# Four of eight k-tile pairs with seven block products in the gate/up projections of a decoder trunk, alternating with pairs of eight

## The chip, the cores and the metric

One Trainium2 chip, one core. The metric is the device time of one execution in microseconds; of several executions of a kernel the median is given. Before the change it is 1897.59 us, the median of three (1898.46, 1897.59 and 1895.63).

## The reference

One layer of a hybrid decoder trunk on 256 tokens of width 2048, all in float32. A combined input projection, three token mixers and their merge come first, then a SwiGLU feed-forward block, a per-layer embedding term and a last norm. The change lies in the feed-forward block alone:

```python
h = rms_norm(x, g_ffn[i])
gate, up = jnp.split(h @ w_gate_up[i], 2, axis=-1)     # 2048 x (2 * 5632)
x = x + (jax.nn.silu(gate) * up) @ w_down[i]           # 5632 x 2048
```

## The kernel before, in words

**Precision.** TensorE multiplies in float32r. Each float32 operand is split in a high and a low part (`whi`, `wlo` for weights), and a product takes three matmuls, high by high, high by low and low by high (`three`, lines 243 to 246). The weights stream from HBM once. ScalarE (ACT) writes the high part (L216) and VectorE (DVE) subtracts it from the raw weights for the low part (L228). There is a second way for the low part (L220, L221): ACT writes the negative of the high part into `wlo`, and a DMA issued on GpSimd's queue (POOL) adds the raw weights to it from HBM, an accumulating transfer of 512 KB, called "an accumulate" below. It saves VectorE a subtraction and costs ACT a copy and the DMA engines a second reading of those weights.

**Quads.** The gate/up projection runs in 11 quads (class `Quad`), numbered 0 to 10 below; the places of the pairs in a quad are numbered from 0 as well. A quad makes 512 columns of gate and the 512 columns of up that belong to them, for both halves of the tokens: a product of 2 x 2 blocks (token half by gate or up) over 16 k-tiles, taken in eight pairs of k-tiles. A pair of kind "o" takes the eight block products, that is 24 matmuls of 128x512, from two split weight pieces. A pair of kind "s" takes the same result with seven products, 21 matmuls, in Winograd's form: sums and differences of the blocks stand for the blocks. Its price is four VectorE additions on the raw weights (L276 and L236) and four split pieces, three whole and one of half size, instead of two. The kinds are in `PAIRS = "soosooso"`: three "s", five "o", 183 matmuls and 8 transposes a quad. The first quad goes through its pairs in an order of its own (`START`), since its last stationary tiles come late. In every "o" pair the piece of the up columns is finished by an accumulate, but for the first four places of the first quad: 52 accumulates in all.

**Groups.** After three quads (in the last group two) come four down products of 12 (8) k-tiles each, on the activations `aT` that the quads of the group left. So a group is three quads of some 42.5 us each and 66 us of down products.

**Buffers and order.** Raw weights have six buffers (`raws`), split pieces seven for each part (`wparts`, in `Flow`: `RAWS, PARTS = 6, 7`). A load starts when an earlier raw tile has been split, and a piece is split when TensorE has done with an earlier piece. The class `Flow` writes each engine's instructions in an order that it plans from costs of its own: 0.681 a product, 1.2 a split, 0.62 an addition, and 8.0 (`ADDED`) that TensorE is to allow an accumulate. `room` decides whether a piece may still be taken, `do_split` allots its buffers and emits. The scheduler beneath may then move instructions of one engine past one another. Each engine works off its own instructions strictly in order. A pool of 13 big tiles (`t8`, 8 KB a partition) holds the two tiles of the residual stream, the eight stationary tiles `st` of the quads, and up to three `aT`. While a group's first quad runs, none of its `aT` is in use yet.

**Evacuation.** The seven accumulators of a quad are merged on ACT and DVE when the next quad starts: a copy (`ga`, L1332), additions on `vx` and `ga` (L506), sigmoids (`gs`, L1345), and then transposes to `aT`. The results of a down product are added to the residual stream `xr` (L506).

Of the kernel before, what the change touches and what calls it, by code (L numbers as in the profile page):

```python
# [11 lines left out]
F32R = mybir.dt.float32r  # L12
# [7 lines left out]
P = 128  # L20
T = 256
D = 2048
NB = 512
# [17 lines left out]
class Group:  # L41
# [6 lines left out]
    def __init__(self, w, kts, c0, n, stat, evac, need=(), pre=None, kind="tok", cost=1.3, key=None):  # L48
        self.w, self.kts, self.c0, self.n = w, list(kts), c0, n
        self.stat, self.evac, self.need, self.pre, self.kind = stat, evac, need, pre, kind  # L50
        self.cost, self.key = cost, key
        self.ps = None
        self.held = []
# [9 lines left out]
class Quad:  # L63
# [6 lines left out]

    def __init__(self, w, c0, c1, pairs, mid, end, order=None, plain=0):
        self.w, self.cs, self.pairs, self.mid, self.end = w, (c0, c1), pairs, mid, end
        self.order = list(order or range(len(pairs)))
        self.plain = plain
        self.ps = {}


# [14 lines left out]
class Piece:  # L94


    def __init__(self, n):
        self.n = n
        self.ops = []
        self.parts = []  # L100
        self.left = 0
# [12 lines left out]
class Flow:  # L114


    RAWS, PARTS = 6, 7
    LAND, GAP, ADDED = 5.0, 1.3, 8.0

    def __init__(self, nc, tc, pools, nm, big, split, quad_parts):  # L120
# [33 lines left out]

    def room(self, piece):
        self.live = [p for p in self.live if p.left]
        return sum(p.n for p in self.live) + piece.n <= self.PARTS

    def next_split(self):

# [10 lines left out]
    def do_split(self, op):  # L171
        if op.piece is not None and op.piece not in self.live:
            p = op.piece
            for part in ("whi", "wlo"):
                p.parts.append([
                    self.pools["wparts"].tile([P, 2, NB], F32R, tag=part, name=self.nm(part)) for _ in range(p.n)
                ])
            self.live.append(p)
        self.emit(self.todo.pop(0))
        for z in op.frees:  # L180
            z.freed = True
            self.slots.append(op.end)
        self.issue()
# [70 lines left out]
    def add_quad(self, g):  # L254
# [2 lines left out]
        first_p, last_p = g.order[0], g.order[-1]  # L257
        for pos, p in enumerate(g.order):
            kind = g.pairs[p]
            r1, r2 = (Load(g.w, 2 * p, c, NB) for c in g.cs)  # L260
            if kind == "s":
                self.loads += [r2, r1]
                pc = [Piece(1) for _ in range(4)]
                x = []

                def new_sum(x=x):
# [9 lines left out]
                        self.nc.vector.tensor_tensor(out=X(0), in0=R2(0), in1=R2(1), op=ALU.add),  # L276
                    ), [], r2,
                )
                b1 = self.split_ops(pc[0], 0, lambda r=r1: r.raw, load=r1)
                t1 = self.add_op(lambda R2=R2: R2(0), lambda R2=R2: R2(0), lambda R1=R1: R1(0), [t3], r1)  # L280
                t2 = self.add_op(lambda X=X: X(1), lambda R2=R2: R2(0), lambda R2=R2: R2(1), [t1], r1)
                self.split_ops(pc[1], 0, lambda r=r2: r.raw, [t1], r2, [r2])
# [15 lines left out]
                              after=(lambda g=g: self.late(g.mid(g, g.ps), g)) if p == last_s and z == "4" else None)  # L298
            else:
                self.loads += [r2, r1]  # L300
                pc = [Piece(1) for _ in range(2)]
                self.split_ops(pc[1], 0, lambda r=r2: r.raw, load=r2, frees=[r2],
                               neg=None if pos < g.plain else g.w[:, 2 * p : 2 * p + 2, g.cs[1] : g.cs[1] + NB])
                self.split_ops(pc[0], 0, lambda r=r1: r.raw, load=r1, frees=[r1])
# [156 lines left out]
def kernel(  # L461
# [284 lines left out]
    w_in_v, w_gu_v, w_dn_v = wv(w_in), wv(w_gate_up), wv(w_down)  # L746
# [510 lines left out]

    PAIRS = "soosooso"  # L1260
    fst = {}

    def quad_stat(p, b, z):
# [160 lines left out]
        return f  # L1424

    NJ = 11
    START = ((1, 2, 0, 4, 3, 5, 6, 7), 4)
    flow.transposes(None, [x_part(3, j) for j in (0, 2)])
    plan = []
    for lo, hi in ((0, 3), (3, 6), (6, 9), (9, NJ)):  # L1430
        for j in range(lo, hi):
            plan.append(Quad(w_gu_v, j * NB, (NJ + j) * NB, PAIRS, quad_mid, quad_end(j), *(START if j == 0 else ())))
        for c in range(4):
            plan.append(Group(w_dn_v, range(4 * lo, 4 * hi), c * NB, NB, blk(aT), ev_down(c, hi == NJ), key="a"))

# [146 lines left out]
```

## Time and profile before

| | us |
|---|---|
| median of three runs | 1897.59 |
| profiled execution | 1896.41 |
| its span in the trace | 1894.6 |
| TensorE busy | 1867.9 (99%) |
| VectorE busy | 1320.2 (70%) |
| ScalarE busy | 1041.1 (55%) |
| quads and down products of the first three groups and the two last quads (1060.77 to 1732.81) | 672.0 |

In the views, PE is TensorE's matmul, PEld its weight load, DVE VectorE, ACT ScalarE, POOL GpSimd's queue and SP the queue of the plain loads. A timeline row has start, duration, engine, line, operation, output <- inputs with their shapes, and in brackets the engine's idle time ahead of it with what ended it. Matmuls are pipelined, so their durations overlap: the distance from one start to the next is what a matmul costs. A row of the windows view has the stretch, its length, each engine's busy time with its instruction count, the granted TensorE clock, the DMA engines' share and the rate in GB/s. A row of a group has busy time and mean ns, then the idle time just ahead and what ended most of it. Times inside the span are from its start. The first quad begins at 1060.77.

### The profile page before, as it was taken

How to read it: one execution, taken by the hardware profiler on the slowest of the kernel's cores; microseconds unless marked ns; L12 is line 12 of the kernel's file. 1: busy time of each engine (PE TensorE's matmuls, PEld its weight loads, DVE VectorE, ACT ScalarE, POOL GpSimd, SP SyncE). 2: the span in 40 equal slices, each digit the busy share in tenths (PEclk: the TensorE clock that was granted, in tenths of full speed). 3: DMA queues.
4: the chain of work that ended last, by engine and by line, in shares of the span. 5: the costliest groups of instructions: out<-in, count | busy, mean ns of one | idle time of the engine just before them, and what ended most of it. 6: DMA issues, size and time to landing. Idle time of an engine off the chain costs nothing.

```text
span 1894.6 us, 23186 instructions
## 1 busy us (share of the span) xinstructions
PE 1867.9 (99%) x8589; PEld 1551.7 (82%) x8589; DVE 1320.2 (70%) x1657; ACT 1041.1 (55%) x1204; POOL 71.7 (4%) x74
## 2 busy tenths in 40 slices
PE   8999999999999999999999999999999999999997
PEld 6888888888888888888888778888888888887887
DVE  6457777668888889655556777758765776676654
ACT  6656556554454435644445666546644665465654
POOL 0000000000000000000000011001100110010000
PEclk9999999999999999999999999999999999999999
DMA  8766556556666656676655599679976997698552
GB/s 311 238 181 186 176 177 190 168 154 178 190 186 193 194 160 211 198 236 189 188 189 167 194 255 263 222 199 259 268 228 192 250 263 239 187 252 277 178 161 95
DMA packets 204401, 390.47 MB, mean 206 GB/s; under 512 B 12432, under 2 KB 21264, under 8 KB 203904
## 3 DMA queue, kind: packets, MB, share of 16 engines
q1 hardware_dynamic: 189248, 358.12, 59.5%
q0 software_dynamic: 15040, 30.87, 9.3%
q8 instruction: 67, 1.10, 0.2%
q14 instruction: 46, 0.38, 0.1%
HBM read 386.85 MB, written 2.10 MB: 205 GB/s over the span
## 4 chain that ended last, share of the span: by engine, by line
PE 92%; DMA 3%; DVE 3%; ACT 1%; issue 1%; SPq 0%; DVEq 0%; ACTq 0%
PE acc L651 17%; PE acc L652 17%; PE acc L650 17%; PE acc L246 12%; PE acc L245 12%; PE acc L244 12%; DMA wlo<-in_w_gate_up_dram 1%; DMA raw<-in_w_gate_up_dram 1%; DVE wlo L228 1%; PE tr L719 1%; PE tr L1287 1%; PE sc L928 1%; DMA x<-in_x_feat_dram 0%; DMA pt<-in_p_feat_dram 0%; DVE raw L236 0%
## 5 line engine op out<-in xcount | busy, mean ns | idle before, releaser
L516 DVE TENSOR_TENSOR wlo<-raw,whi 128x1024 fp32r<-128x1024 f32 (+2 forms) x378 | 450.0, 1196 | 293.9 <-ACT whi L515 293.3
L515 ACT ACTIVATE whi<-raw 128x1024 fp32r<-128x1024 f32 (+2 forms) x378 | 391.2, 1037 | 465.1 <-PE acc L652 391.8
L216 ACT ACTIVATE whi<-raw 128x1024 fp32r<-128x1024 f32 (+1 forms) x333 | 332.3, 1006 | 301.4 <-PE acc L246 267.0
L650 PE MATMUL acc<-whi,hhi 128*128 128x512 f32 (+1 forms) x1120 | 432.7, 387 | 5.5 <-ACT whi L515 5.5
L651 PE MATMUL acc<-wlo,hhi 128*128 128x512 f32 (+1 forms) x1120 | 430.1, 384 | 0.5 <-DVE wlo L516 0.5
L652 PE MATMUL acc<-whi,hlo 128*128 128x512 f32 (+1 forms) x1120 | 430.1, 384 | 0.0
L228 DVE TENSOR_TENSOR wlo<-raw,whi 128x1024 fp32r<-128x1024 f32 (+1 forms) x281 | 318.1, 1144 | 155.6 <-ACT whi L216 154.7
L245 PE MATMUL acc<-wlo,st 128*128 128x512 f32 x671 | 262.1, 391 | 4.1 <-DMA wlo<-in_w_gate_up_dram 3.6
L244 PE MATMUL acc<-whi,st 128*128 128x512 f32 x671 | 262.0, 393 | 1.6 <-DVE xr L506 1.5
L246 PE MATMUL acc<-whi,st 128*128 128x512 f32 x671 | 261.5, 391 | 0.0
L650 PEld LDWEIGHTS acc<-whi,hhi 128*128 128x128 f32 x1120 | 210.8, 188 | 46.5 <-ACT whi L515 5.9
L651 PEld LDWEIGHTS acc<-wlo,hhi 128*128 128x128 f32 x1120 | 210.9, 188 | 41.9 <-DVE wlo L516 1.4
L652 PEld LDWEIGHTS acc<-whi,hlo 128*128 128x128 f32 x1120 | 210.7, 188 | 41.3
L245 PEld LDWEIGHTS acc<-wlo,st 128*128 128x128 f32 x671 | 126.3, 188 | 32.0 <-DMA wlo<-in_w_gate_up_dram 5.0
L244 PEld LDWEIGHTS acc<-whi,st 128*128 128x128 f32 x671 | 126.3, 188 | 29.1 <-DVE xr L506 1.5
L246 PEld LDWEIGHTS acc<-whi,st 128*128 128x128 f32 x671 | 126.4, 188 | 26.4
L244 PE MATMUL acc<-whi,aT 128*128 128x512 f32 x352 | 138.3, 393 | 1.5 <-ACT aT L515 1.5
L245 PE MATMUL acc<-wlo,aT 128*128 128x512 f32 x352 | 137.2, 390 | 0.0
L246 PE MATMUL acc<-whi,aT 128*128 128x512 f32 x352 | 136.6, 390 | 0.0
L509 DVE SCALAR_TENSOR_TENSOR cv<-uT,vec,cv 128x255 f32<-128x255 f32 (+15 forms) x240 | 110.8, 466 | 4.8
L221 POOL DMA_DIRECT2D wlo<-in_w_gate_up_dram x52 | 62.6, 1204 | 819.9 <-ACT wlo L220 485.8
L244 PEld LDWEIGHTS acc<-whi,aT 128*128 128x128 f32 x352 | 66.2, 188 | 15.5 <-ACT aT L515 2.1
(276 smaller groups left out, 2073.7 us busy)
## 6 DMA issues: line engine op xcount, KB each, us to landing
raw<-in_w_in_dram SPq DMA_DIRECT2D x262, 512.0 KB, 3.7
raw<-in_w_gate_up_dram SPq DMA_DIRECT2D x176, 512.0 KB, 5.3
raw<-in_w_down_dram SPq DMA_DIRECT2D x88, 512.0 KB, 5.1
wlo<-in_w_gate_up_dram POOLq DMA_DIRECT2D x52, 512.0 KB, 8.2
raw<-in_w_gla_out_dram SPq DMA_DIRECT2D x32, 512.0 KB, 3.6
raw<-in_w_o_dram SPq DMA_DIRECT2D x32, 512.0 KB, 4.0
raw<-in_w_ple_gate_dram SPq DMA_DIRECT2D x24, 512.0 KB, 3.6
raw<-in_w_sc_out_dram SPq DMA_DIRECT2D x16, 512.0 KB, 4.3
```

Of the source, the lines that this page charges most:

```text
L216: a = self._op("A", cost * 0.88, lambda: nc.scalar.activation(out=hi(), in_=src(), func=AF.Copy), deps, load, piece, frees if neg else ())
L221: nc.gpsimd.dma_start(out=lo(), in_=neg, accum_op=ALU.add)
L228: lambda: nc.vector.tensor_tensor(out=lo(), in0=src(), in1=hi().bitcast(F32), op=ALU.subtract),
L244: pe.matmul(o, lhsT=s[0], rhs=w[0], start=start, stop=False)
L245: pe.matmul(o, lhsT=s[0], rhs=w[1], start=False, stop=False)
L246: pe.matmul(o, lhsT=s[1], rhs=w[0], start=False, stop=stop)
L509: dve.scalar_tensor_tensor(out=o, in0=a, scalar=s, in1=b, op0=op0, op1=op1)
L515: a = act.activation(out=hi, in_=src, func=AF.Copy)
L516: b = dve.tensor_tensor(out=lo, in0=src, in1=hi.bitcast(F32), op=ALU.subtract)
L650: pe.matmul(o, lhsT=shi[:, hs], rhs=whi, start=st, stop=False)
L651: pe.matmul(o, lhsT=shi[:, hs], rhs=wlo, start=False, stop=False)
L652: pe.matmul(o, lhsT=slo[:, hs], rhs=whi, start=False, stop=sp)
```

## The change

`PAIRS` becomes "sosososo": four "s" and four "o" pairs, alternating, 180 matmuls a quad. In every quad but the first, the "s" pairs at places 0 and 2 finish their first piece (the gate columns) by an accumulate instead of VectorE's subtraction (`NEG`). The first quad gets another order of pairs and no accumulate at all (`START`). So there are 60 accumulates, six in each of ten quads. `Piece` gets a number `may`: when the seven ordinary buffers are full, a piece can take a big tile (`wp`, high and low part in one) as long as fewer pieces than `may` are in such tiles. Quads of a group get 3, 2 and 1 for it (`lo + 3 - j`), the first quad of a group from its third place on only.

```diff
-    PAIRS = "soosooso"
+    PAIRS = "sosososo"
...
-    START = ((1, 2, 0, 4, 3, 5, 6, 7), 4)
+    START = ((1, 3, 0, 2, 5, 4, 6, 7), 8)
...
-            plan.append(Quad(w_gu_v, j * NB, (NJ + j) * NB, PAIRS, quad_mid, quad_end(j), *(START if j == 0 else ())))
+            plan.append(Quad(w_gu_v, j * NB, (NJ + j) * NB, PAIRS, quad_mid, quad_end(j), *(START if j == 0 else (None, 0)), lo + 3 - j))
...
+    NEG = (0, 2)
...
-        return sum(p.n for p in self.live) + piece.n <= self.PARTS
+        return self.held(False) + piece.n <= self.PARTS or self.held(True) < piece.may
+
+    def held(self, extra):
+        return sum(p.n for p in self.live if p.extra == extra)
...
+            p.extra = self.held(False) + p.n > self.PARTS
+            if p.extra:
+                b = self.big("wp", (P, 2, 2, NB), F32R)
+                p.parts = [[b[:, 0, :, :]], [b[:, 1, :, :]]]
...
+            may = g.spare if pos > 1 or g.spare < 3 else 0
...
-                pc = [Piece(1) for _ in range(4)]
+                pc = [Piece(1, may) for _ in range(4)]
...
-                b1 = self.split_ops(pc[0], 0, lambda r=r1: r.raw, load=r1)
+                b1 = self.split_ops(pc[0], 0, lambda r=r1: r.raw, load=r1,
+                                    neg=g.w[:, 2 * p : 2 * p + 2, g.cs[0] : g.cs[0] + NB] if pos in self.NEG and not g.plain else None)
```

Three places of the order show what moves. Numbers behind a name only tell tiles apart; line numbers after the change are higher by 11 to 13.

VectorE in the first quad. Before, an "s" pair (from L276 on) with an "o" pair's splits on its two sides:

```order
L228 TENSOR_TENSOR wlo_8453<-raw_8329,whi_8452 128x1024
L228 TENSOR_TENSOR wlo_8459<-raw_8335,whi_8458 128x1024
L276 TENSOR_TENSOR sum_8478<-raw_8365 128x512
L228 TENSOR_TENSOR wlo_8481<-raw_8378,whi_8480 128x1024
L236 TENSOR_TENSOR raw_8365<-raw_8365,raw_8378 128x512
L236 TENSOR_TENSOR sum_8478<-raw_8365 128x512
L236 TENSOR_TENSOR raw_8378<-raw_8378,sum_8478 128x512
L228 TENSOR_TENSOR wlo_8499<-raw_8365,whi_8498 128x1024
L228 TENSOR_TENSOR wlo_8518<-sum_8478,whi_8517 128x1024
L228 TENSOR_TENSOR wlo_8522<-raw_8378,whi_8521 128x512
L276 TENSOR_TENSOR sum_8561<-raw_8456 128x512
```

Now two "s" pairs stand behind one another (the end of the first is shown), and then both splits of an "o" pair:

```order
L239 TENSOR_TENSOR wlo_8442<-sum_8408,whi_8441 128x1024
L239 TENSOR_TENSOR wlo_8450<-raw_8321,whi_8449 128x512
L288 TENSOR_TENSOR sum_8455<-raw_8332 128x512
L239 TENSOR_TENSOR wlo_8458<-raw_8338,whi_8457 128x1024
L247 TENSOR_TENSOR raw_8332<-raw_8332,raw_8338 128x512
L247 TENSOR_TENSOR sum_8455<-raw_8332 128x512
L247 TENSOR_TENSOR raw_8338<-raw_8338,sum_8455 128x512
L239 TENSOR_TENSOR wlo_8478<-raw_8332,whi_8477 128x1024
L239 TENSOR_TENSOR wlo_8491<-sum_8455,whi_8490 128x1024
L239 TENSOR_TENSOR wlo_8498<-raw_8338,whi_8497 128x512
L239 TENSOR_TENSOR wlo_8504<-raw_8368,whi_8503 128x1024
L239 TENSOR_TENSOR wlo_8510<-raw_8381,whi_8509 128x1024
```

The first quad has one such pair more than before, and as many "o" splits on VectorE.

ScalarE ahead of the first accumulate. Before, it belongs to the sixth pair of the first quad (the last row is its negative copy):

```order
L216 ACTIVATE whi_8498<-raw_8365 128x1024
L216 ACTIVATE whi_8517<-sum_8478 128x1024
L216 ACTIVATE whi_8521<-raw_8378 128x512
L216 ACTIVATE whi_8533<-raw_8435 128x1024
L216 ACTIVATE whi_8546<-raw_8450 128x1024
L220 ACTIVATE wlo_8534<-whi_8533 128x1024
```

Now it is the first pair of the second quad, behind the half piece of the first quad's seventh pair (`whi_8625`, which reads the last addition), both pieces of its eighth, and the copy of a finished bank:

```order
L227 ACTIVATE whi_8618<-sum_8585 128x1024
L227 ACTIVATE whi_8625<-raw_8501 128x512
L227 ACTIVATE whi_8631<-raw_8507 128x1024
L227 ACTIVATE whi_8637<-raw_8519 128x1024
L227 ACTIVATE whi_8657<-raw_8580 128x1024
L1345 ACTIVATE ga_8670<-acc_8465 128x512
L231 ACTIVATE wlo_8658<-whi_8657 128x1024
```

The first accumulate has moved some four pairs later, to the start of the second quad.

ScalarE around the start of the third quad of the third group. Before, two accumulates (`wlo_12133` and `wlo_12184`), the second with two other splits between its own split and its copy:

```order
L216 ACTIVATE whi_12132<-raw_12003 128x1024
L220 ACTIVATE wlo_12133<-whi_12132 128x1024
L216 ACTIVATE whi_12161<-raw_12026 128x1024
L1345 ACTIVATE gs_12110<-ga_12103,y_8278 128x512 x2
L216 ACTIVATE whi_12183<-raw_12031 128x1024
L216 ACTIVATE whi_12194<-raw_12051 128x1024
L216 ACTIVATE whi_12208<-raw_12123 128x1024
L220 ACTIVATE wlo_12184<-whi_12183 128x1024
```

Now two as well, each with one split between (`wlo_12172` is that of place 1, `wlo_12235` that of place 2):

```order
L227 ACTIVATE whi_12171<-raw_12066 128x1024
L227 ACTIVATE whi_12192<-raw_12089 128x1024
L231 ACTIVATE wlo_12172<-whi_12171 128x1024
L1358 ACTIVATE gs_12189<-ga_12182,y_8281 128x512 x2
L227 ACTIVATE whi_12234<-raw_12113 128x1024
L227 ACTIVATE whi_12271<-raw_12094 128x1024
L231 ACTIVATE wlo_12235<-whi_12234 128x1024
```

The copy of place 1 now stands behind another split (`whi_12192`), where before the copy followed its own split at once; that of place 2 has one split ahead of it instead of two. In the whole program TensorE has 33 instructions less, VectorE 64 more rows, ScalarE 28 more and POOL 8 more; SP's are as many.

More of the change, by code (lines that the diff above doesn't have):

```diff
@@ L63, with __init__ @@
 class Quad:
-    def __init__(self, w, c0, c1, pairs, mid, end, order=None, plain=0):
+    def __init__(self, w, c0, c1, pairs, mid, end, order=None, plain=0, spare=0):
         self.w, self.cs, self.pairs, self.mid, self.end = w, (c0, c1), pairs, mid, end
@@ L76, in __init__ @@
         self.plain = plain
+        self.spare = spare
         self.ps = {}
@@ L94, with __init__ @@
 class Piece:
-    def __init__(self, n):
+    def __init__(self, n, may=0):
         self.n = n
+        self.may, self.extra = may, False
         self.ops = []
@@ L173, in do_split @@
             p = op.piece
[L174 to L177, printed above, removed]
+            p.extra = self.held(False) + p.n > self.PARTS
+            if p.extra:
+                b = self.big("wp", (P, 2, 2, NB), F32R)
+                p.parts = [[b[:, 0, :, :]], [b[:, 1, :, :]]]
+            else:
+                for part in ("whi", "wlo"):
+                    p.parts.append([
+                        self.pools["wparts"].tile([P, 2, NB], F32R, tag=part, name=self.nm(part)) for _ in range(p.n)
+                    ])
             self.live.append(p)
@@ L300, in add_quad @@
                 self.loads += [r2, r1]
-                pc = [Piece(1) for _ in range(2)]
+                pc = [Piece(1, may) for _ in range(2)]
                 self.split_ops(pc[1], 0, lambda r=r2: r.raw, load=r2, frees=[r2],
```

## The prediction

> **What bounds the kernel now.** I read the page first, then busy time by stage, then TensorE's timeline in the one stage where it falls short.
>
> ```profile
> span 1894.6 us, 23186 instructions
> PE 92%; DMA 3%; DVE 3%; ACT 1%; issue 1%; SPq 0%; DVEq 0%; ACTq 0%
> L245 PE MATMUL acc<-wlo,st 128*128 128x512 f32 x671 | 262.1, 391 | 4.1 <-DMA wlo<-in_w_gate_up_dram 3.6
> L244 PE MATMUL acc<-whi,st 128*128 128x512 f32 x671 | 262.0, 393 | 1.6 <-DVE xr L506 1.5
> ```
>
> TensorE (PE) makes 92% of the chain, so whatever shortens its stream shortens the kernel, as long as nothing else starts to end waits. The third row is the change's own ground: 671 is 11 quads of 61 steps, one low-part matmul each, and 3.6 us is what PE waited there for accumulated low parts. The last row has 1.5 us in which PE waited for VectorE's residual adds. Busy time in four quads and in 20 us of one:
>
> ```profile
> core 0: us, PE busy (x) PEld busy (x) DVE busy (x) ACT busy (x) POOL busy (x), PEclk, DMA share, GB/s
> 1060.77:1108.76 47.99, 44.44 (x188) 35.68 (x188) 42.15 (x59) 35.95 (x46) 3.65 (x3) 0.96 0.74 220
> 1108.76:1151.18 42.42, 42.42 (x192) 35.14 (x191) 34.05 (x43) 30.04 (x33) 5.98 (x5) 1.00 0.95 262
> 1302.20:1344.80 42.60, 42.60 (x192) 35.05 (x191) 34.42 (x44) 29.16 (x32) 6.01 (x5) 1.00 0.94 260
> 1538.65:1581.82 43.17, 42.75 (x192) 35.06 (x191) 31.79 (x38) 28.36 (x30) 4.81 (x4) 1.00 0.96 267
> 1120.00:1140.00 20.00, 20.00 (x90) 16.57 (x89) 13.34 (x17) 13.04 (x13) 3.58 (x3) 1.00 1.01 295
> ```
>
> Quads 1, 4 and 8 take 42.4 to 43.2 us with PE busy throughout; VectorE (DVE) idles 8.2 us in quad 4. Quad 0 takes 48.0, and its DVE is busy 42.15. Why:
>
> ```profile
> 1085.99 0.39 PE L244 MATMUL acc<-whi,st 128*128 128x512 f32 x1
> ...
> 1090.75 0.39 PE L244 MATMUL acc<-whi,st 128*128 128x512 f32 x1
> 1094.32 0.50 PE L245 MATMUL acc<-wlo,st 128*128 128x512 f32 x1 [3.19 <-DMA wlo<-in_w_gate_up_dram]
> ...
> 1095.54 0.63 PE L246 MATMUL acc<-whi,st 128*128 128x512 f32 x1
> 1095.96 0.63 PE L244 MATMUL acc<-whi,st 128*128 128x512 f32 x1
> ...
> 1098.52 0.42 PE L244 MATMUL acc<-whi,st 128*128 128x512 f32 x1
> ```
>
> From 1085.99 to 1090.75 stand 21 matmuls: 0.2267 us each, start to start. Then PE idles 3.19 us for one accumulate, and afterwards starts lie 0.42 apart (the granted clock halves) up to 1098.52, which costs 8 x 0.195 = 1.6. So quad 0 loses 4.8 us to one late landing. The chain has the landings:
>
> ```profile
> 1085.44 8.84 DMA wlo<-in_w_gate_up_dram
> ...
> 1156.41 9.08 DMA wlo<-in_w_gate_up_dram
> ...
> 1543.88 9.41 DMA wlo<-in_w_gate_up_dram
> ```
>
> **Term 1, the products.** Each quad loses one eighth product: three matmuls; 11 quads, 33 matmuls, all on the path: 33 x 0.2267 = -7.5 us. A quad's stream becomes 42.4 - 0.7 = 41.7 us.
>
> **What the added kind costs DVE and ScalarE (ACT).** DVE in the first quad:
>
> ```profile
> 1077.17 0.68 DVE L276 TENSOR_TENSOR sum<-raw 128x512 f32<-128x512 f32 x1
> 1077.77 1.22 DVE L228 TENSOR_TENSOR wlo<-raw,whi 128x1024 fp32r<-128x1024 f32 x1
> 1078.91 0.68 DVE L236 TENSOR_TENSOR raw<-raw,raw 128x512 f32<-128x512 f32 x1
> ...
> 1083.83 0.68 DVE L276 TENSOR_TENSOR sum<-raw 128x512 f32<-128x512 f32 x1
> ...
> 1091.39 0.68 DVE L276 TENSOR_TENSOR sum<-raw 128x512 f32<-128x512 f32 x1
> ```
>
> Between the first two sums lies one whole seven-product pair, back to back: 6.66 us; one full split takes 1.14 (1077.77 to 1078.91). A later quad gets +6.66 for the pair, -1.14 for the eight-product pair that it replaces, and -2.28 for the two splits (positions 0 and 2) that now end in an accumulate: +3.2. DVE in quad 4 goes from 34.4 to 37.6 of 41.7 us. ACT gets 3.5 more activations, loses 3 and adds 2 copies: +2.6, to 31.8 (1.06 us each, a row of term 2). Both are hidden beside PE, cost nothing, and would cost what they exceed 41.7 if their own waits grew.
>
> **Term 2, the first quad.** No accumulate is left in it, so its 3.19 and 1.6 us go. In their place DVE has 6.66 us more: four seven-product pairs instead of three, and eight plain splits as before. Before, DVE reached quad 1's first sum at 1091.39 without a pause; now at 1098.1. The last add of position 6 stands five splits ahead (four of 1.14, one of 0.6): 1092.9. ScalarE's order then has, behind that add, a half split, two full ones, the split for quad 1's first accumulate, the copy of a bank, and the negative copy:
>
> ```profile
> 1537.10 1.32 ACT L1345 ACTIVATE gs<-ga,y 128x512 f32<-128x512 f32 x2
> 1538.85 1.07 ACT L216 ACTIVATE whi<-raw 128x1024 fp32r<-128x1024 f32 x1 [0.43 <-PE acc L246]
> 1540.21 1.06 ACT L216 ACTIVATE whi<-raw 128x1024 fp32r<-128x1024 f32 x1 [0.29 <-PE acc L246]
> 1541.57 1.06 ACT L216 ACTIVATE whi<-raw 128x1024 fp32r<-128x1024 f32 x1 [0.30 <-PE acc L246]
> 1542.54 1.04 ACT L220 ACTIVATE wlo<-whi 128x1024 fp32r<-128x1024 f32 x1
> ```
>
> With 1.06 for a full one, 0.6 for each half-size one (an estimate from the 1.06), and 1.34 from the negative copy's start to the issue (1542.54 to 1543.88), the accumulate is issued at about 1092.9 + 0.6 + 3.2 + 0.6 + 1.34 = 1098.6 and lands, 8.84 later, at 1107.5. PE would want it at its second matmul of quad 1: 1060.77 + 48.0 - 4.8 - 0.7 + 0.2 = 1103.5. So it idles 4.0 us and pays the half clock again: 5.6 us against 4.8. Term 2 = +0.8. The stall is not removed, it moves from the sixth pair of quad 0 to the first pair of quad 1. Its ends: -4.8 (DVE or the landing 4 us faster than these rows, no stall), and +3 (DVE also pauses for ACT). I take the middle because every duration in it is a row of this very stage.
>
> **Term 3, margins of the other accumulates.** A piece is split when a buffer of the seven comes free. For an eight-product pair's accumulate that is two pairs and half of the third ahead of its use: (21 + 24 + 12) x 0.2267 = 12.9 us; for position 0 or 2 it is (21 + 24 + 6) x 0.2267 = 11.6. ACT takes two activations and the issue, 2.4, so 10.5 and 9.2 remain for a landing. In quad 1:
>
> ```profile
> q1 hardware_dynamic: 4392, 8.48, 58.6%
> q0 software_dynamic: 1360, 2.62, 36.2%
> ...
> wlo<-in_w_gate_up_dram POOLq DMA_DIRECT2D x5, 512.0 KB, 8.4
> ```
>
> 8.4 median, and up to 9.41 above: 1.1 us to spare before, about nothing now where no big tile helps. By the order the big tiles serve only from the second group of quads on, and there mostly the first two quads of a group; quads 1 and 2 and the third quads of groups two and three run on seven buffers, or seven and one.
>
> ```profile
> 1105.70 1.28 ACT L1345 ACT_TABLE_LOAD   x1
> ```
>
> - Quad 1: behind the first accumulate's copy (done by 1098.3) ACT's order has two splits, the table load, two sigmoids, a half split, three splits and then the second one's copy: 1098.3 + 2.1 + 1.3 + 1.3 + 0.6 + 3.2 + 1.34 = 1108.1, and 1.5 more (an estimate, between 0 and 3) where the sigmoids wait for DVE: issued at 1109.6, landing (8.84) at 1118.4. PE wants it 37 matmuls after the first, 1107.5 + 1.6 + 8.4 = 1117.5: +0.9; the third one queues behind it, +0.4. Together +1.3, ends 0 and +3.
> - The three third quads: in quad 8 now the copy starts two splits after its own split, is issued 5.2 us into the quad and lands at 14.6. After, position 2 is wanted at (21 + 24 + 6) x 0.2267 + 0.9 for the transposes = 12.4 us, with one split between instead of two: issued at 3.8, landing 8.4 to 9.4: up to 0.8 late. Position 1's is queued behind a split that waits for the last pair of the quad ahead: issued near -0.2, wanted at 7.9, 0.3 to 1.3 late. A stall at one gives time to the other: 0.6 per quad, 1.8, less the 0.4 that PE waits so already (3.6 - 3.19): +1.4, ends -0.4 and +5.
>
> **Term 4, where a group begins.** In DVE's order the residual adds of the last down product stand behind adds of the second seven-product pair, which wait for its load:
>
> ```profile
> 1257.92 0.69 DVE L236 TENSOR_TENSOR raw<-raw,raw 128x512 f32<-128x512 f32 x1 [3.75 <-DMA raw<-in_w_gate_up_dram]
> ```
>
> That pair was the fourth of a quad and is now the third, so its loads are the fifth and sixth instead of the seventh and eighth, and six buffers hold them all: they start without waiting for a buffer of the quad's own. Of the 1.5 us that PE waits for residual adds I take 1.0 as gone: -1.0, ends -1.5 and +1 (another wait ahead of the same adds).
>
> The big tiles themselves cost nothing: each is one that a later aT takes, its first use lies 12 us into its quad, and the old aT is read for the last time before the quad starts. If ACT met one not yet free, everything queued on ACT behind it would wait with it.
>
> **Sum**, against the profiled 1896.4 us (span 1894.6 and 1.8 around it): -7.5 + 0.8 + 1.3 + 1.4 - 1.0 = -5.0. The median of the three runs is 1897.6, the profiled run lies 1.2 under it and inside their spread; against the median the forecast is 1892.6.
>
> **A rule that bears on the landings.** Two stretches, one with DVE full, one not, each with its landing:
>
> ```profile
> wlo<-in_w_gate_up_dram POOLq DMA_DIRECT2D x2, 512.0 KB, 9.0
> 1298.00:1308.00 10.00, 10.00 (x45) 8.07 (x44) 9.83 (x15) 7.40 (x9) 2.41 (x2) 1.00 0.93 260
> ```
>
> ```profile
> wlo<-in_w_gate_up_dram POOLq DMA_DIRECT2D x1, 512.0 KB, 7.0
> 1567.00:1578.00 11.00, 11.00 (x51) 9.09 (x50) 6.17 (x6) 8.13 (x9) 1.20 (x1) 1.00 0.88 245
> ```
>
> DVE busy 98%: 9.0 us; 56%: 7.0, at nearly the same DMA share. A busier DVE goes with later landings, and the change makes it busier. The Trainium skill, SBUF — State Buffer, section "Who interferes with whom", infers that VectorE's tensor_tensor does not hold up descriptors that GpSimd writes. By that the landing would stay at the quiet figure, and the sum would be without the +1.4 of the third quads: -6.4. The trace speaks against it, as far as two stretches can.
>
> **Rivals.**
> - *Full gain*: the accumulate of quad 1 comes in time. Then -7.5 - 4.8, and +1.4 of third quads: about -11, 1886.6. For it: DVE is the only thing late there. Against: the sum of rows, by which it is 4.0 us late. Chance 0.17.
> - *The gain is eaten*: as DVE fills, the landing goes to 9.3 and over everywhere; positions 0 and 2 then miss by 0.5 each in some four quads that have no big tile for them, +4 more: -1, 1896.6. For it: the two stretches. Against: the big tiles give the other quads more time. Chance 0.20.
> - *Slower, DMA becomes the bound*: in quad 1 a load takes 0.586 x 42.42 / 16 = 1.55 us of all engines and an accumulate 0.362 x 42.42 / 5 = 3.07. With six accumulates a quad asks 16 x 1.55 + 6 x 3.07 = 43.2 us of 41.7. Were these shares real occupancy, ten quads would take 43.2: 10 x 0.7 more than now, with term 2 about +8, 1905.6. It decides once a quad's DMA work passes 41.7. Against: at a share of 1.01 PE was busy 20.00 of 20.00 us and 295 GB/s went through, while 22 transfers of 524 KB in 41.7 us ask 277. Chance 0.15.
> - *It does not do what it says*: the order has the 33 matmuls less and 60 accumulates for 52, but no big tile in the first three quads; that is in the terms, no case of its own.
>
> **How the numbers follow.** 0.2% is 3.8 us, about what a measurement here can tell from no change. The forecast has 0.48, with a range of its own from -8 to -2, most of it past -3.8: 0.35 faster, 0.13 no change. Full gain adds 0.17 faster; the eaten gain 0.20, of it 0.16 no change and 0.04 slower (its upper end is the +3 and +5 of terms 2 and 3); the DMA bound 0.15 slower. Faster 0.52, same 0.29, slower 0.19. The range leaves out half of the full gain and most of the DMA case, under 2 in 10: 1887.5 to 1901.
>
> **What would show it.** Right: 660 low-part matmuls of the quads instead of 671; quad 0 near 43 us without a wait over 1 us; a wait of 3 to 5 us at quad 1's second matmul, with the clock halved behind it; waits under 1 us in the third quads; DVE near 37 us in a full quad. Wrong: no such wait in quad 1 (full gain); landings over 9.5 and many short waits at low-part matmuls (eaten); quads over 42.5 us with a DMA share of 1 (slower).

## The result, and the profile after

The changed kernel takes 1913.4 us (median of four, 1908.3 to 1915.9) against 1896.6 us for the kernel before (median of four): 1.0078 times the time, interval 1.0065 to 1.0091. It is slower by 17 us; 1892.6 had been predicted, with a range to 1901. The profiled run took 1915.9.

The page of the changed kernel, in the rows that answer to those of before:

```profile
span 1914.0 us, 23287 instructions
...
L256 PE MATMUL acc<-wlo,st 128*128 128x512 f32 x576 | 229.2, 399 | 10.8 <-DMA wlo<-in_w_gate_up_dram 10.8
L255 PE MATMUL acc<-whi,st 128*128 128x512 f32 x576 | 227.4, 400 | 10.8 <-DVE vx L519 10.5
```

PE waited 3.6 us for accumulates and now waits 10.8. In the second row 10.5 us of waiting for VectorE's `vx`, the additions that empty a quad's accumulators, are new; before the change that row had 1.5 us for residual adds. (With 84 low-part matmuls that read big tiles, the 576 make the expected 660.) The windows view of the changed kernel, quads 0, 1, 3, 4 and 5:

```profile
core 0: us, PE busy (x) PEld busy (x) DVE busy (x) ACT busy (x) POOL busy (x), PEclk, DMA share, GB/s
1061.34:1103.87 42.53, 42.31 (x184) 33.70 (x185) 42.05 (x60) 30.03 (x39) 1.24 (x1) 1.00 0.64 193
1103.87:1157.39 53.52, 46.83 (x189) 37.03 (x188) 42.11 (x56) 36.87 (x42) 8.42 (x7) 0.90 0.93 246
...
1268.39:1309.23 40.84, 40.84 (x181) 33.63 (x180) 28.76 (x36) 28.08 (x30) 7.05 (x6) 1.00 0.98 269
1309.23:1357.49 48.26, 44.73 (x189) 36.32 (x189) 39.79 (x51) 30.68 (x35) 6.18 (x6) 0.93 0.89 247
1357.49:1399.10 41.61, 41.61 (x189) 34.27 (x188) 34.24 (x42) 30.90 (x34) 4.84 (x4) 1.00 0.96 264
```

Quads 3 and 5 are as short as the products promise (40.84 is about 180 x 0.2267, in a quad without transposes; 41.61 one with them). Quad 0 has lost its stall. Quad 1 takes 53.5 us instead of 42.4, and quad 4 takes 48.3 instead of 42.6, as do 7 (48.6) and 10 (47.2), the other second quads of a group. Against before, quads 0 and 1 together are 5.6 us longer, quads 4, 7 and 10 16.6, and the six others 1.9 shorter: 20.3, where the span grew by 19.4.

TensorE at the start of quad 4, in the timeline:

```profile
1311.81 0.39 PE L257 MATMUL acc<-whi,st 128*128 128x512 f32 x1
1315.73 0.79 PE L255 MATMUL acc<-whi,st 128*128 128x512 f32 x1 [3.53 <-DVE vx L519]
1316.32 0.63 PE L256 MATMUL acc<-wlo,st 128*128 128x512 f32 x1
```

It wants the fifth accumulator of the new quad, whose bank the quad ahead still holds, and afterwards runs at half clock (starts 0.43 us apart). VectorE in the 14 us up to that point:

```profile
1302.05 0.69 DVE L288 TENSOR_TENSOR sum<-raw 128x512 f32<-128x512 f32 x1 [3.23 <-DMA raw<-in_w_gate_up_dram]
1305.74 0.69 DVE L247 TENSOR_TENSOR raw<-raw,raw 128x512 f32<-128x512 f32 x1 [3.00 <-DMA raw<-in_w_gate_up_dram]
...
1307.68 0.68 DVE L519 TENSOR_TENSOR vx<-acc,ga 128x512 f32<-128x512 f32 x1
...
1310.14 0.68 DVE L519 TENSOR_TENSOR ga<-ga,acc 128x512 f32<-128x512 f32 x1
...
1314.40 1.28 DVE L519 TENSOR_TENSOR vx<-vx,acc 128x512 f32<-128x512 f32 x2
```

VectorE idles 6.2 us for two loads of raw weights, with the evacuation standing behind them. Its first addition reads what ScalarE copied out of a bank. The copy in the changed kernel, and that addition before the change (where quad 4 starts at 1302.20):

```profile
1301.80 0.58 ACT L1345 ACTIVATE ga<-acc 128x512 f32<-128x512 f32 x1
```

```profile
1298.04 0.68 DVE L506 TENSOR_TENSOR vx<-acc,ga 128x512 f32<-128x512 f32 x1
```

The copy ends at 1302.38, but the addition runs only at 1307.68, 1.6 us ahead of the new quad; before the change it ran 4.2 us ahead. (So the first 3.2 of the 6.2 us passed before the copy was there.) The additions that wait belong to the third pair of the quad that has not begun: with a piece in a big tile, the order lets the splits run that far ahead, and there the first additions come in front of the evacuation; the first, second and eighth experiments below test this. The additions that free PE's bank end at 1315.68; PE goes on at 1315.73.

Quad 1, TensorE's first wait and a later one:

```profile
1103.87 0.39 PE L255 MATMUL acc<-whi,st 128*128 128x512 f32 x1
1108.17 0.79 PE L256 MATMUL acc<-wlo,st 128*128 128x512 f32 x1 [3.91 <-DMA wlo<-in_w_gate_up_dram]
...
1132.74 0.50 PE L256 MATMUL acc<-wlo,st 128*128 128x512 f32 x1 [2.34 <-DMA wlo<-in_w_gate_up_dram]
1133.08 0.40 PE L257 MATMUL acc<-whi,st 128*128 128x512 f32 x1
1133.32 0.46 PE L255 MATMUL acc<-whi,st 128*128 128x512 f32 x1
1133.58 0.63 PE L256 MATMUL acc<-wlo,st 128*128 128x512 f32 x1
```

The first is the wait that the prediction moved here. The second, at the fourth place, it did not have.

### The profile page after: what moved, and what is told of

Same layout as the page of the kernel before. It is cut to its first block, busy times and chain, and to the rows that moved or that the text cites. A ratio compares the mean times of both kernels' runs of the same rounds, so it can differ in the third digit from the quotient of the medians.

```text
span 1914.0 us, 23287 instructions
## 1 busy us (share of the span) xinstructions
PE 1872.4 (98%) x8556; PEld 1550.9 (81%) x8556; DVE 1357.4 (71%) x1718; ACT 1061.6 (55%) x1234; POOL 81.4 (4%) x82
## 5 line engine op out<-in xcount | busy, mean ns | idle before, releaser
L227 ACT ACTIVATE whi<-raw 128x1024 fp32r<-128x1024 f32 (+1 forms) x320 | 311.5, 987 | 261.7 <-PE acc L257 211.7
L239 DVE TENSOR_TENSOR wlo<-raw,whi 128x1024 fp32r<-128x1024 f32 (+1 forms) x269 | 299.4, 1118 | 138.6 <-ACT whi L227 137.9
L664 PEld LDWEIGHTS acc<-wlo,hhi 128*128 128x128 f32 x1120 | 210.9, 188 | 41.8 <-DVE wlo L529 1.4
L256 PE MATMUL acc<-wlo,st 128*128 128x512 f32 x576 | 229.2, 399 | 10.8 <-DMA wlo<-in_w_gate_up_dram 10.8
L255 PE MATMUL acc<-whi,st 128*128 128x512 f32 x576 | 227.4, 400 | 10.8 <-DVE vx L519 10.5
L257 PE MATMUL acc<-whi,st 128*128 128x512 f32 x576 | 227.7, 397 | 0.0
L255 PEld LDWEIGHTS acc<-whi,st 128*128 128x128 f32 x576 | 110.3, 192 | 37.9 <-DVE vx L519 12.9
L256 PEld LDWEIGHTS acc<-wlo,st 128*128 128x128 f32 x576 | 110.6, 192 | 37.1 <-DMA wlo<-in_w_gate_up_dram 14.4
L257 PEld LDWEIGHTS acc<-whi,st 128*128 128x128 f32 x576 | 110.9, 192 | 23.4
```

Of the source, the lines that this page charges most:

```text
L227: a = self._op("A", cost * 0.88, lambda: nc.scalar.activation(out=hi(), in_=src(), func=AF.Copy), deps, load, piece, frees if neg else ())
L239: lambda: nc.vector.tensor_tensor(out=lo(), in0=src(), in1=hi().bitcast(F32), op=ALU.subtract),
L255: pe.matmul(o, lhsT=s[0], rhs=w[0], start=start, stop=False)
L256: pe.matmul(o, lhsT=s[0], rhs=w[1], start=False, stop=False)
L257: pe.matmul(o, lhsT=s[1], rhs=w[0], start=False, stop=stop)
L664: pe.matmul(o, lhsT=shi[:, hs], rhs=wlo, start=False, stop=False)
```

## The experiments

Theory O (order): the waits for a bank come from VectorE's order, in which big tiles let additions that wait for loads stand ahead of the evacuation. Theory L (local lack): the waits for accumulates come from VectorE's work in the first third of a quad, and for quad 1 from its work in quad 0; the accumulates are issued late, not landed slowly. Against both (called M or D): the transfers fill the DMA engines. Each ratio is to the kernel before on the same chip. The numbers in the headings are those by which the expectations count. Times of quads and waits are read from one profiled execution of each kernel, which lay from 4 us below its median (first) to 6 us above it (fourth), so a difference of a few us between two profiles is no proof by itself. "From start to start" counts a wait as what the distance between two matmuls has over 0.2267.

**1: without big tiles.**

```diff
-..., *(START if j == 0 else (None, 0)), lo + 3 - j))
+..., *(START if j == 0 else (None, 0)), 0))
```

> The changed kernel with no piece ever in a big tile (every quad gets 0 for it); products, accumulates and the first quad's order stay. Theory O (order): in quads 4, 7 and 10 VectorE's evacuation stands in its order behind the additions of the third pair of the new quad, which wait for their loads, and only the big tiles let the splits run that far ahead. Without them the three quads lose their waits for a bank (48.3, 48.6 and 47.2 us become 42 +- 1, about -18), the first quads of the groups lose their lead (40.8 becomes 41.7, +2.7), and some accumulates come up to 1 us late: 1897 to 1902. Theory M (transfers): the six accumulates of a quad fill the DMA engines and make loads late; they are all still there, so the waits stay, quads 4, 7 and 10 over 45 us, and the total is within 4 us of 1913.

1904.0 us, 1.0029 (1.0020 to 1.0039), 2 us above the range of theory O. Quads 4, 7 and 10 took 42.6, 42.7 and 44.6, without one wait for a bank, with all accumulates in place: theory O, and not M. But the first quads kept their 40.85 to 41.0, so that lead was not the big tiles' work, and most later quads now waited 0.7 to 2.9 us (from start to start) at the fourth place's accumulate.

**2: all tiles, additions tied.** The planner holds a quad's third pair back until the banks are read, and a copy of one column makes it binding.

```diff
+        if op.hold is not None and op.hold.out < 11:
+            return None
...
                         new_sum(),
+                        tie and self.nc.vector.tensor_copy(out=X(0)[:, 0:1], in_=tie.v[:, 1, 0:1]),
```

> The changed kernel with all its transfers, big tiles and splits, but the additions of a quad's third pair tied behind the evacuation of the quad ahead: a copy of one column from vx (after the additions that free six of the seven banks) into the sum tile, so that VectorE can't have them in front. Theory O: the waits for a bank at the start of quads 4, 7 and 10 (3.7, 3.7 and 3.3 us, and the half clock behind each) fall under 0.5 us and these quads take 42 +- 1; the rest stays: 1896 +- 3. Theory M: the loads are as late as before, so PE waits for the third pair's pieces in place of the bank, and the total stays over 1907.

1901.6 us, 1.0017 (1.0007 to 1.0026): 5 us above the expected 1896, but 12 below the change. Quads 4, 7 and 10 took 43.5, 42.3 and 41.8, again with no wait for a bank:

```profile
1308.06:1351.54 43.48, 42.63 (x189) 34.34 (x188) 36.88 (x49) 29.44 (x34) 6.49 (x6) 1.00 0.94 259
1502.74:1545.04 42.30, 42.16 (x190) 34.42 (x189) 36.09 (x48) 29.25 (x33) 6.02 (x5) 1.00 0.95 258
1695.41:1737.23 41.82, 41.82 (x189) 34.23 (x187) 36.02 (x46) 27.86 (x31) 3.79 (x4) 1.00 0.94 271
```

The big tiles and all transfers are still there; the order did it.

**8: big tiles on the old pairs** (`PAIRS`, `START` of before, `NEG = ()`).

> The kernel before with the big tiles alone: three seven-product pairs, its own first quad, no accumulate in a seven-product pair. If the big tiles harm by what they let run ahead, with any pairs: waits of 1 to 3 us for a bank at the start of quads 4, 7 and 10, 1903 or more. If it takes the third pair's additions ahead of the evacuation (in the old kinds the next seven-product pair is at place 3, and ends later): no such wait, within 3 us of before.

1903.0 us, 1.0017 (1.0001 to 1.0033): the first alternative. PE waited 1.2 to 2.0 us for a bank in quads 4, 7, 8 and 10 (8 had not been expected). Ahead of quad 4 two additions of a seven-product pair wait 2.58 and 2.38 us for loads in VectorE's order here too. The big tiles harm by themselves; with the new pairs the waits are twice as long.

**3: quad 1 without accumulates in its seven-product pairs, and 4: the products alone** (`NEG = ()` and no big tiles). In the third, `g.w2` is false for quads 0 and 1.

```diff
-... if pos in self.NEG and not g.plain else None)
+... if pos in self.NEG and not g.plain and g.w2 else None)
```

> The changed kernel, but the seven-product pairs of quad 1 (places 0 and 2) are split without an accumulate. Theory: the wait of 4.1 us at quad 1's second matmul and the 1.6 us of half clock go, and the later accumulates of quad 1 are issued earlier as ACT has two copies less, so the wait of 2.5 us at its fourth place goes at least in part: -5 to -9, 1904 to 1908. Rival: the lateness is VectorE's (the splits of quad 0 end late), so the accumulate of the second place is late instead by as much: within 2 us of 1913.

> The four seven-product pairs and the first quad's order alone: no accumulate in a seven-product pair, no big tiles; every eight-product pair but those of the first quad keeps its accumulate. VectorE has 34.4 + 6.66 - 1.14 = 39.9 us of work in a quad of 41.7. Theory O: no wait of over 1 us for a bank in quads 4, 7 and 10, no wait at quad 1's first pair; 11 x 0.68 us less for the products and quad 0's 4.8: 1886 to 1892. Rival (VectorE is the limit, which is why the two accumulates were added): quads of 43 us and more with waits for VectorE's low parts, 1897 or more.

Both expectations failed: 1914.7 us, 1.0086 (1.0071 to 1.0101), with quad 1 at 56.0; and 1915.9 us, 1.0085 (1.0069 to 1.0102), with quad 1 at 57.5 and waits of 3.9 and 4.0 us at the fourth place in quads 4 and 7. Fewer accumulates, longer waits for the accumulates that are left: so it is not their number that delays them. Each one taken away gives VectorE 1.14 us more to do, which points to VectorE.

**5: a light evacuation.** The first 18 us of quad 4, before the change (first) and in the first experiment:

```profile
1302.20:1320.20 18.00, 18.00 (x84) 14.70 (x83) 16.43 (x22) 11.74 (x13) 2.41 (x2) 1.00 0.95 254
```

```profile
1305.58:1323.58 18.00, 18.00 (x85) 14.89 (x84) 17.96 (x25) 13.08 (x15) 2.41 (x2) 1.00 1.03 276
```

VectorE is busy 17.96 of 18.00 us there, before the change 16.43. ScalarE, GpSimd's queue and TensorE in that stretch of the first experiment, one fence each:

```profile
1310.27 1.06 ACT L227 ACTIVATE whi<-raw 128x1024 fp32r<-128x1024 f32 x1 [2.33 <-DVE raw L247]
```

```profile
1317.55 1.20 POOL L232 DMA_DIRECT2D wlo<-in_w_gate_up_dram  x1 [8.10 <-ACT wlo L231]
```

```profile
1325.16 0.50 PE L256 MATMUL acc<-wlo,st 128*128 128x512 f32 x1 [0.56 <-DMA wlo<-in_w_gate_up_dram]
```

ScalarE's splits of the third pair wait for VectorE's additions, which stand behind the evacuation; the fourth place's split and copy stand behind those on ScalarE. The accumulate is issued 7.6 us ahead of its matmul. Before the change the two issues of such a stretch, at 1304.86 and 1315.70, stood about 11 us ahead of theirs (1316.47 and 1326.67 in the timeline). The next experiment leaves out the four multiplications of the evacuation.

```diff
-                    rm(0),
...
-                    rm(1),
...
-                    last(1),
...
-            ops = [flow.op("D", 0.7, lambda: tt(v[:, 0, :], v[:, 0, :], ps["3"], ALU.add)), last(0)]
+            ops = [flow.op("D", 0.7, lambda: tt(v[:, 0, :], v[:, 0, :], ps["3"], ALU.add))]
```

> The changed kernel without big tiles (as in the first experiment), and in it the four multiplications of each quad's evacuation left out on VectorE (the gate's product with its sigmoid and with up, 4 x 0.67 = 2.7 us a quad; so the activations are not the reference's). Theory L (VectorE is short of time at the start of a quad): the fourth place's accumulate is issued late because ACT's splits of the third pair wait for additions that stand behind the evacuation; 2.7 us less there bring the issue 2 to 3 us forward, and the waits at the fourth place (0.7 to 1.9 us in quads 4, 5, 7, 8, 2.9 in quad 10) fall under 0.3: quads of 41.6 to 42.0. Rival D (the accumulates land late because the DMA engines are full): same transfers, same waits, quads 42.6 to 43.5.

1894.3 us, 0.9978 (0.9968 to 0.9989). Quads 2 to 10 had not one wait over 0.5 us; two of them:

```profile
1306.96:1348.73 41.77, 41.77 (x189) 34.57 (x188) 34.67 (x44) 32.16 (x35) 7.22 (x6) 1.00 1.01 276
1348.73:1390.25 41.52, 41.52 (x188) 34.38 (x187) 33.85 (x41) 30.54 (x33) 4.84 (x4) 1.00 0.99 289
```

Six accumulates a quad, a DMA share of 1, and PE busy throughout: theory L, and no limit of transfers. The accumulates landed no sooner here (median of the run 8.9 us, in the first experiment 8.5). Quad 1 stayed at 53.4.

**6: the same work, spread otherwise** (`PAIRS = "soososso"`, `NEG = (0, 3)`, the first quad's order 1, 2, 0, 3, 4, 5, 6, 7).

> Four seven-product pairs as in the change, at places 0, 3, 5 and 6 instead of 0, 2, 4 and 6 (accumulates of such pairs at 0 and 3; the first quad's eight products first, no accumulate in it), and no big tiles. VectorE has the same work in a quad, but one seven-product pair less in its first 15 us, beside the evacuation. Theory L: no wait over 0.5 us at the fourth place in quads 4, 5, 7, 8, 10; these take 41.6 to 42.3; total 4 to 8 us under the first experiment's 1904. Rival (all of VectorE's work counts, 37 of 41.7 us): the waits move to another place, within 2 us of 1904.

1919.2 us, 1.0113 (1.0092 to 1.0134), worse than either. PE now waited 1.3 to 2.1 us in the first 5 us of nearly every quad from quad 2 on, in all 6.4 us for the evacuation's `vx`, 4.9 for residual adds, and some 5 for the first accumulate in quads 2, 5 and 8. The rival is half right: the waits move, and they grow as well. That two such pairs in a row leave VectorE late for what follows is likely, but no run shows it alone.

**9: part of that relief with nothing left out, Silu on ScalarE.**

```diff
-... act.activation(out=s[:, h, :], in_=m[:, h, :], func=AF.Sigmoid, scale=rr("f", h)))
+... act.activation(out=m[:, h, :], in_=m[:, h, :], func=AF.Silu, scale=rr("f", h)))
...
-                    rm(0),
...
-                    rm(1),
```

> The changed kernel without big tiles, with the gate's sigmoid and its multiplication on VectorE taken as one Silu on ACT: two multiplications less in each quad's evacuation (2 x 0.67 = 1.35 us, half of what the fifth experiment left out), and the result stays the reference's. Theory L: the fourth place's accumulate is issued 1 to 1.5 us earlier than in the first experiment, so waits of 0.7 go and those of 1.5 to 2.9 fall by 1 to 1.5; quads 4, 5, 7, 8, 10 lose 1 us each on the average: 1899 +- 2. Rival D (landings): no change against the first experiment's 1904, within 2 us.

1897.9 us, 1.0000 (0.9990 to 1.0009), as expected. Quads 2 to 10 fell from 383.0 us to 376.4 (382.0 before the change, 372.6 with the light evacuation). Quad 1 stayed bad, 55.3.

**7 and 10: accumulates in the first quad.** The seventh, whose edit is shown, is on the base of the tied kernel; the tenth is without big tiles and has `pos > 5`.

```diff
-... if pos in self.NEG and not g.plain else None)
+... if (pos > 4 if g.plain else pos in self.NEG) else None)
...
-    START = ((1, 3, 0, 2, 5, 4, 6, 7), 8)
+    START = ((1, 3, 0, 2, 5, 4, 6, 7), 7)
```

> The second experiment (additions tied behind the evacuation) with VectorE relieved in the first quad: the eight-product pair at place 7 and the seven-product pairs at places 5 and 6 finish one piece by an accumulate, which takes three subtractions of 1.14 us off VectorE there. Theory (what makes quad 1's first accumulate late is VectorE's work in quad 0, 42.05 of 42.5 us): it is issued 2 to 3.4 us earlier than 1100.7, the wait of 4.2 us falls to 1 to 2, that of 2.0 at the fourth place falls too, quad 1 from 52.4 to 45 to 48: 1894 to 1898. Rival (three more accumulates queue ahead of it): the wait stays at 4 or grows, over 1900.

> The changed kernel without big tiles, with two accumulates in the first quad, at places 6 (seven-product) and 7 (eight-product), so that VectorE has two subtractions of 1.14 us less there. The seventh experiment's accumulate at place 5 came 3.8 us late; place 6 is wanted 4.8 us later. Theory (VectorE's work in quad 0 delays what follows): quad 0 at 43 to 44 with a wait of 0 to 1, quad 1's first accumulate issued 1.5 to 2.3 us before 1100.4, its wait 4.1 falls to about 2 and the half clock behind it goes: quads 0 and 1 together 89 to 91 (93.3 in the first experiment), 1900 to 1902. Rival (accumulates queue one behind another): together 93 or more, 1904 or more.

1902.1 us, 1.0020 (1.0010 to 1.0029), and 1903.0, 1.0027 (1.0018 to 1.0037). Both missed their expectation. Quad 1 got shorter (45.7 and 46.9) and quad 0 longer (49.7 and 50.0, with waits of 3.8 and 5.0 us at its own first accumulate): together 95.4 and 96.9, against 95.0 and 93.3 without. At each of the three places tried, the first accumulate is late. In quad 0 VectorE is busy 42.05 of 42.5 us, so the splits have hardly any lead, and an accumulate takes some 8 to 9 us to land.

**11: the ninth and the tenth together.**

> Both of the two before in one kernel. If the two lacks of VectorE's time (in quad 0, and at the start of the later quads) are separate, their gains add: 1904 - 5 - 3 = 1896 +- 2, at or just under the kernel before (1898.6). If one hides in the other: 1898 to 1901.

1898.2 us, 0.9996 (0.9987 to 1.0005): the gains do not add. On either base the accumulates in quad 0 gain nothing that these runs can tell (1.0027 against 1.0029 in the first experiment, 0.9996 against 1.0000 in the ninth). In the profiled executions quads 0 and 1 are 3.2 us shorter together than in the ninth, and quads 2 to 10 4.0 longer; what made those longer no run separates.

**13: a light first quad.** The ninth kernel without the second and the fourth addition of each seven-product pair of quad 0.

```diff
-                t1 = self.add_op(
+                t1 = t3 if g.plain else self.add_op(
...
-                t4 = self.add_op(
+                t4 = t2 if g.plain else self.add_op(
```

> The ninth experiment (Silu, no big tiles) with two of the four additions of each seven-product pair of the first quad left out (8 x 0.6 = 4.8 us of VectorE; those pairs' products are then not the reference's). Theory (VectorE's work in quad 0 sets when quad 1's first accumulate is issued): the issue comes 3 to 5 us earlier than 1100.4, the wait of 4.4 us at quad 1's second matmul goes under 1, and of the 3.2 us at its fourth place at least half goes: quad 1 from 55.3 to 42 to 48, 1885 to 1891. Rival (the landing itself, or ACT's order, sets it): the wait at the second matmul stays over 3 and quad 1 over 50, 1895 or more.

1890.0 us, 0.9955 (0.9940 to 0.9970). The first accumulate in GpSimd's timeline, in the ninth kernel and here:

```profile
1100.63 1.24 POOL L232 DMA_DIRECT2D wlo<-in_w_gate_up_dram  x1 [262.03 <-ACT wlo L231]
```

```profile
1096.18 1.24 POOL L232 DMA_DIRECT2D wlo<-in_w_gate_up_dram  x1 [257.58 <-PE acc L257]
```

4.45 us earlier for 4.8 us of additions left out; the wait of 4.4 us at quad 1's second matmul is gone and quad 1 takes 46.9. VectorE's work in quad 0 sets it, as the prediction had it; with that much less of it, the issue's last wait is for PE. Of the 3.2 us at the fourth place 2.5 remain, where at least half had been expected to go.

**12: tied and Silu.**

> The second experiment (big tiles used, additions tied behind the evacuation) and the Silu of the ninth together, with the changed kernel's own first quad. If the two lacks are separate, quads 2 to 10 take what the ninth has (376.4 us together) less what the second has under the first (381.2 against 383.0): some 374.5; quads 0 and 1 stay at 95 to 98: 1896 +- 2, at or under the kernel before (1898.5). If the tie costs once the evacuation is short: 1898 to 1901.

1902.4 us, 1.0024 (1.0014 to 1.0034): a miss, the last alternative and more. Quads 2 to 10 took 380.4 us; the fourth place waits 1.2 to 1.6 us in quads 4, 5 and 8, where the ninth kernel has none or 0.6. That the held-back third pair is itself late once the evacuation is short would fit this, but no run shows it alone.

**14 and 15: the additions on GpSimd.** In quad 0, of each seven-product pair the first sum and the last addition, and in the fifteenth the second and the last (on the base of the ninth).

```diff
+        e = self.nc.gpsimd if pool else self.nc.vector
         return self._op(
-            "D", 0.62, lambda: self.nc.vector.tensor_tensor(
+            "G" if pool else "D", 1.3 if pool else 0.62, lambda: e.tensor_tensor(
```

> The ninth experiment (Silu, no big tiles) with two of the four additions of each of the first quad's seven-product pairs (the first sum and the last one) on GpSimd, which has nothing else to do there; the result stays the reference's. What one such addition takes on GpSimd no run has shown yet; VectorE's takes 0.68. If up to 1.5 us each, VectorE is relieved by 4.8 us as in the thirteenth: quad 1's first accumulate issued 3 us or more earlier than 1100.6, 1889 to 1894, under the kernel before (1898.5). If 3 us or more, ACT's split of the half piece waits for it and quad 0 grows: 1898 or more.

> As the run before, with the second and the last addition (the two that the thirteenth left out) on GpSimd. The second stands between the first sum and the third addition, both on VectorE, so each pair waits once for GpSimd and back: 0 to 3 us later than the run before, 1890 to 1897; VectorE's busy time in quad 0 is the same, so if the two differ by over 2 us, it is the chain between the engines and not VectorE's busy time that counts.

1899.9 us, 1.0003 (0.9994 to 1.0012), the second alternative, and 1903.5, 1.0026 (1.0016 to 1.0036), a miss. An addition takes 1.3 to 2.2 us on GpSimd, and VectorE next to it gets slower; the pair of rows shows one of each, GpSimd's and VectorE's, from the fourteenth:

```profile
1070.83 1.41 POOL L248 TENSOR_TENSOR raw<-raw,sum 128x512 f32<-128x512 f32 x1 [9.96 <-DVE wlo L239]
```

```profile
1071.00 2.33 DVE L239 TENSOR_TENSOR wlo<-raw,whi 128x1024 fp32r<-128x1024 f32 x1
```

A subtraction that takes 1.22 us alone took 2.33. Quad 0 went to 49.3 and 50.7. No kernel that leaves nothing out beat the kernel before by more than the measurement can tell.

## Why the prediction was wrong, point by point

A gain of 5.0 us was forecast, and the span grew by 19.4. Of the 24.4 us between the two, 18.6 lie in quads 4, 7 and 10 (16.6 longer, where fewer matmuls were to make them 2.0 shorter), 4.9 in quads 0 and 1 and 2.8 in the third quads of the groups; the rest came out 1.9 better.

- **The big tiles cost nothing: wrong, and the step that failed.** I asked whether a tile was free and whether ScalarE would wait for one. What they cost is what they let run ahead of what: the third pair's additions ahead of the evacuation, on VectorE. PE's three waits (idle 3.53, 3.53 and 3.16 us) are 10.2 of the 10.5 us in the group row; with the half clock after each, quads 4, 7 and 10 are 16.6 us longer. Both experiments that take this order away have no such wait. My order rows of the place looked at ScalarE only.
- **VectorE's added work is hidden: wrong as a mean over the quad.** The sum was about right: +3.2 in ten quads and +6.66 in the first make 38.7, and VectorE's busy time went from 1320.2 to 1357.4, 37.2 more (single quads differ: 28.8 in quad 3, 39.8 in 4, 34.2 in 5). But VectorE has the evacuation to do in the first third of a quad, and now two seven-product pairs beside it instead of one: 17.96 of 18.00 us in the first experiment. The light evacuation shows it.
- **Term 1, -7.5: right.** Quads without a wait take 41.5 to 41.8 us, and the first ones of groups 40.84.
- **Term 2, +0.8: right in mechanism, in size partly by luck.** Idle 4.0 forecast, 3.91 measured; half clock behind it; quad 0 at 42.5, "near 43" forecast. But the issue came at 1100.4 instead of 1098.6, and this was made up by a landing of 7.8 us instead of 8.84 and by quad 1 starting 0.6 later than assumed. The light first quad shows the cause.
- **Term 3, +1.3 in quad 1 and +1.4 in the third quads: the size was wrong in quad 1.** It counted the second and third accumulate. The second wait, 2.34 us with another stretch of half clock, is at the fourth place, which was not in the sum; with 0.8 at the other two, and the half clock, it comes to 5 to 6 us. In the trace ScalarE's `aT` copy waits 4.9 us for PE's transposes, VectorE's `aT` subtraction for the copy, and the third pair's additions stand behind it: the first wait comes back through the transposes. That is read from the trace; no run separates it. Of the third quads, 2 is 1.9 us longer, 8 is 0.9 longer and 5 is 0.7 shorter, though each has lost 0.7 us of matmuls: 4.2 against the 1.4 forecast, inside that term's end of 5. (The prediction has quad 8 busy throughout before the change; its row has 42.75 of 43.17.)
- **Term 4, -1.0: right**, the residual adds' waits at the start of quads 6 and 9 (1.0 and 0.6 us start to start) are gone.
- **The landings.** I held the two stretches (9.0 us with VectorE full, 7.0 without) against the Trainium skill, SBUF — State Buffer, "Who interferes with whom", which infers that tensor_tensor does not hold up GpSimd's descriptors. In the 18 us with VectorE busy 17.96, the DMA view of the first experiment has this row (the last figure is the median landing):

```profile
wlo<-in_w_gate_up_dram POOLq DMA_DIRECT2D x2, 512.0 KB, 7.6
```

  So the page stands here and my reading of two stretches does not. Over whole runs the median landing is 8.2 us before the change, 8.5 in the first experiment and 8.9 with the light evacuation, which has no such waits in quads 2 to 10: the accumulates are late because they are issued late, and land only a little slower.
- **The rivals.** "Transfers become the bound" had the right sign with the wrong mechanism: quads of 41.5 us ran at a share of 0.99 and 289 GB/s. None of the rivals was an order in which an engine's own waiting stands ahead of what PE needs.

## What to carry to other kernels

More buffers for running ahead can change the order in which an in-order engine does its work: ask what will stand ahead of the instruction that frees the consumer's accumulators, and what that waits for. A busy share over a stage hides a stretch in which an engine is full; sum its work over the stretch in which its consumer asks for it. And an operation that takes longer to arrive but spares an engine (here an accumulate with 9 us for a subtraction of 1.14) needs a lead that an engine at its limit does not have.

## What the runs showed of the hardware

- Half clock did not follow from the length of an idle stretch. After 2.34 us it came, 0.8 us behind the restart (the row at 1133.58 above), and lasted to 1136.97, 3.4 us. In the same execution 2.66 us of idle time in quad 2 brought none:

```profile
1179.08 0.50 PE L256 MATMUL acc<-wlo,st 128*128 128x512 f32 x1 [2.66 <-DMA wlo<-in_w_gate_up_dram]
1179.42 0.40 PE L257 MATMUL acc<-whi,st 128*128 128x512 f32 x1
```

  In all the runs here, from the first quad on, no idle stretch of up to 1.73 us had half clock behind it and each one of 3.5 us and more had; in between both occur, with it after 1.78 us (seventh experiment, quad 8) and without it after 3.34 (twelfth, quad 1).

  The Trainium skill, TensorE: Matmul & The Clock Gate, Part 1, tells of a free-running window of some 3.4 us; the 3.4 us and the chance in it agree. By the same part the clock falls after at least one idle window of about 3.4 us; the traces do not agree, since 2.34 and 1.78 were enough.
- VectorE's subtraction of 128x1024 takes 1.22 us alone and took 2.33 beside an addition on GpSimd (rows above; the sixteen such subtractions on raw weights in quad 0 took 1.57 on the average). The Trainium skill, SBUF — State Buffer, "Who interferes with whom", says that a VectorE instruction with two inputs in SBUF contends with a GpSimd instruction that reads SBUF; the runs agree. That the same instructions leave GpSimd's DMA issues alone (landing 7.6) agrees as well.
